# Retention heads: score products with the decay emitted ahead of the lo parts, and GpSimd's weight sums in halves

## The chip, the cores and the metric

The kernel runs on one core of one Trainium2 chip. The metric is the device time of one execution in microseconds (us). "Before" is the median of three runs. A profile is of one execution, with the name of each tile that an instruction reads and writes, and the line of the kernel that issued it. The engines are called PE (TensorE, matmuls; PEld its weight loads), DVE (VectorE), ACT (ScalarE), POOL (GpSimd) and SP (SyncE, which issues most DMAs).

## The reference, cut to what matters

One layer of a decoder: a normalised input of 512 tokens and 16 meta tokens goes through a combined projection `w_in`; four retention heads and sixteen stick-breaking heads run side by side; their gated outputs are merged and projected, and a SwiGLU FFN follows. All is float32. The change lies in the retention heads:

```python
scores = jnp.einsum('bhncd,bhnsd->bhncs', qc, kc) * decay[:, None]
inner = jnp.einsum('bhncs,bhnse->bhnce', scores, vc)
...
y_ret = head_groupnorm(retention_chunkwise(q_r, k_r, heads(rv, RET_HEADS)))
y_ret = (jax.nn.silu(rg.astype(jnp.float32)) * merge_heads(y_ret)).astype(dtype) @ w_ret_out
```

Each head has keys and queries of width 256 and values and a gate of width 512. The kernel computes a head's scores over the whole sequence at once, with one decay table for the causal triangle, in place of the reference's chunks with a carried state.

## The kernel before, in words

Matmuls of near-float32 accuracy are made of three products. Every operand is split into a hi part (`split`, L98: ACT copies it to the matmul format, L99) and a lo part (`lo_of`, L95: DVE subtracts the hi part from the source, L96); PE multiplies hi by hi, hi by lo and lo by hi. So for each weight or activation a DVE subtraction follows an ACT copy; all of them have the lines L99 and L96, and are told apart by their tiles: `wh`, `wl` are weights, `sh`, `sl` scores, `smt` the scores of the meta tokens.

The large projections of the retention heads use a scheme of seven products of half-size blocks in place of eight (`seven`, L260, numbered 0 to 6). It needs sums of the weights' quarters. `tok_quarters` (L230) loads a head's gate or value weights as two DMA tiles `raw` of 128x2048, splits the quarters, and has POOL form four sums of 128x1024 elements (L252 to L255): `y` and `x` go to tiles named `st`, the other two are made in place. They are split in turn (`wl<-st`, `wl<-raw`). It is called so for the gate of all four heads and for the values of heads 1 to 3; the values of head 0 are summed in place by other lines (L244 to L247). The results of the seven products are added into `ub` by DVE: L271, L274, L277 (which reads product 4, in a bank of the pool `b`) and L282.

A head's order in the program is: `ret_qk` (queries and keys, rotated), `tok_quarters` of the gate, `ret_scores`, `ret_gate`, `ret_pv` (scores times values, group norm, gating), `ret_T` (transposes), then `rv_proj` of the next head (its `tok_quarters` and seven products) and `ret_out`. In `ret_scores` each score block is a group of six matmuls into a PSUM bank `pb`; first the 16 meta rows (512 columns), then four blocks `j` of 128 rows with 512, 384, 256 and 128 columns. DVE multiplies the bank by the decay table into a tile `tm` (L941 for the meta rows, L953 for the blocks), and `tm` is split into hi and lo. In `ret_pv` the group of matmuls for token block `i` begins with the meta rows (`rvm`, `smt`) and then uses the blocks 0 to `i`.

Two rings set limits here. Score blocks, product 4 of the gate, and the groups of `ret_pv` share the two banks of the pool `b`. The tiles `tm` share a ring of three buffers, `rt`, with the temporaries of the rotation and of the group norm.

The order within each engine's queue is drawn up when the program is built: a planner goes through the instructions with its own estimate of their times and gives each engine, among those that are ready, the one emitted first. It fills a free engine with later work, so weights of the next head are split between the steps of this one. A few parts (the stick-breaking stage and the final product) are pinned to the order of the program; the retention heads are not. Once built, each engine runs its queue strictly in order.

Of the kernel before, what the change touches and what calls it, by code (L numbers as in the profile page):

```python
# [10 lines left out]
F32 = mybir.dt.float32  # L11
F32R = mybir.dt.float32r
AF = mybir.ActivationFunctionType
ALU = mybir.AluOpType
PSUM = bass.MemoryType.PSUM

P = 128
NM = 16
T = 512
L = NM + T  # L20
NT = T // P
# [13 lines left out]
def hybrid_block(  # L35
# [18 lines left out]
    nc = tc.nc  # L54
    x, out = x[0], out[0]
# [15 lines left out]
    def bank_b():  # L71
        return ps_b.tile([P, 512], F32, tag="b", name="pb")
# [16 lines left out]
    def mm(*args, **kw):  # L89
        return keep(nc.tensor.matmul(*args, **kw))  # L90
# [4 lines left out]
    def lo_of(lo, src, hi):  # L95
        nc.vector.tensor_tensor(lo, src, hi.bitcast(F32), op=ALU.subtract)  # L96

    def split(hi, lo, src):  # L98
        ins = nc.scalar.activation(hi, src, AF.Copy)  # L99
        if split_in_order[0]:  # L100
            tc.keep_in_program_order(ins)
        lo_of(lo, src, hi)
# [43 lines left out]
    H, KH = T // 2, KD // 2  # L146
# [43 lines left out]
    def wun_split(v):  # L190
        wh = wun.tile([P, v.shape[1], v.shape[2]], F32R, tag="wh", name="wh")
        wl = wun.tile([P, v.shape[1], v.shape[2]], F32R, tag="wl", name="wl")
        split(wh, wl, v)
        return wh, wl
# [35 lines left out]
    def tok_quarters(src, sums=None):  # L230

        raws = []
        for i in range(2):
            raw = wraw.tile([P, KH, 512], F32, tag="raw", name="raw")
            nc.sync.dma_start(raw, src[KH * P * i : KH * P * (i + 1), :].rearrange("(k p) c -> p k c", p=P))
            raws.append(raw)
        A11, A21 = raws[0][:, :, 0:256], raws[0][:, :, 256:]
        A12, A22 = raws[1][:, :, 0:256], raws[1][:, :, 256:]
        u = {}
        u["a11"] = wun_split(A11)  # L240
        u["a12"] = wun_split(A12)
        if sums is None:
            u["a22"] = wun_split(A22)
            nc.gpsimd.tensor_tensor(A22, A21, A22, op=ALU.add)  # L244
            nc.gpsimd.tensor_tensor(A21, A11, A21, op=ALU.subtract)
            nc.gpsimd.tensor_tensor(A11, A22, A11, op=ALU.subtract)
            nc.gpsimd.tensor_tensor(A12, A12, A11, op=ALU.subtract)  # L247
            u["s2"], u["s3"], u["s1"], u["s4"] = [wun_split(a) for a in (A11, A21, A22, A12)]
            return u
        x = sums.tile([P, KH, 256], F32, tag="st", name="st")  # L250
        y = sums.tile([P, KH, 256], F32, tag="st", name="st")
        nc.gpsimd.tensor_tensor(y, A11, A21, op=ALU.subtract)  # L252
        nc.gpsimd.tensor_tensor(A21, A21, A22, op=ALU.add)
        nc.gpsimd.tensor_tensor(x, A21, A11, op=ALU.subtract)  # L254
        nc.gpsimd.tensor_tensor(A12, A12, x, op=ALU.subtract)  # L255
        u["s2"], u["s3"], u["s1"] = wun_split(x), wun_split(y), wun_split(A21)
        u["s4"], u["a22"] = wun_split(A12), wun_split(A22)
        return u
# [563 lines left out]
    RT = 3  # L822
    s4 = s4c.enter_context(tc.tile_pool(name="s4", bufs=2, side=RS, reuse_waits="tile"))
# [11 lines left out]
    smt = s4.tile([80, T], F32R, name="smt", bufs=1)  # L835
# [26 lines left out]
    def rv_proj(h):  # L862
        u = tok_quarters(w_in[:, O_RV + DV * h : O_RV + DV * (h + 1)], s4 if h else None)
        ub = s4.tile([P, 4, 512], F32, tag="ub", name="ub", bufs=1)
        vs = s4.tile([P, L], F32, tag="rt", name="vs", bufs=RT)[:NM, :DV]

        def meta_part(n):

            c = 0 if n == 1 else 1
            ps, cs = bank_b()[:48, :256], slice(256 * c, 256 * (c + 1))  # L870
            ws = ((xm[:, 0:KH], u["a11"]), (xm[:, KH:KD], u["a12"])) if c == 0 else ((xm[:, 0:KH], u["s1"]), (xm2, u["a22"]))
            for i, (m, w) in enumerate(ws):
                for k in range(KH):
                    for j in range(2):
                        mm(ps, m[:, k, :], w[j][:, k, :], start=(i + j + k == 0), stop=(i == 1 and j == 1 and k == KH - 1))
            nc.scalar.activation(vs[:, cs], ps[32:48], AF.Copy)
            nc.vector.tensor_tensor(vs[:, cs], ps[0:16], vs[:, cs], op=ALU.add)

        tok_seven(u, tokens, ub, after=meta_part)
        vh = s4.tile([P, NT, DV], F32R, tag="vh", name="vh", bufs=1)  # L880
        vl = s4.tile([P, NT, DV], F32R, tag="vl", name="vl", bufs=1)
        for q in range(4):
            c, t = q // 2, q % 2
            dst = lambda v: v[:, 2 * t : 2 * t + 2, 256 * c : 256 * (c + 1)]
            split(dst(vh), dst(vl), ub[:, q, :].rearrange("p (a b) -> p a b", a=2))
        split(rvm[0:16, :], rvm[64:80, :], vs)
        nc.scalar.activation(rvm[32:48, :], rvm[0:16, :].bitcast(F32), AF.Copy)
        return [(vh[:, j, :], vl[:, j, :]) for j in range(NT)]
# [20 lines left out]
    def ret_qk(h):  # L909
        uq = feat_units(w_in[:, O_RQ + DK * h : O_RQ + DK * (h + 1)])  # L910
        pq = bank_a()
        for e in range(2):
            feat_mm(pq[:, e, :], uq[e], xtok, ltok)
        q = [(qk_tile(), qk_tile()) for _ in range(2)]
        idf = lambda t: t[:, :T]
        rotate(pq[:, 0, :], pq[:, 1, :], cosT[:, NM:], sinT[:, NM:], idf, [(a[:, :T], b[:, :T]) for a, b in q])
        uk = feat_units(w_in[:, O_RK + DK * h : O_RK + DK * (h + 1)])
        pks = []
        for e in range(2):
            pk = bank_a()  # L920
            for i in range(2):
                cs = slice(264 * i, 264 * (i + 1))
                feat_mm(pk[:, i, :264], uk[e], lambda k: hT[:, k, cs], lambda k: hL[:, k, cs])
            pks.append(pk[:, :, :264])
        k = [(qk_tile(), qk_tile()) for _ in range(2)]
        two = lambda t: t.rearrange("p (a b) -> p a b", a=2)
        rotate(pks[0], pks[1], two(cosT), two(sinT), two, [(two(a), two(b)) for a, b in k])
        return q, k

    def ret_scores(h, q, k):  # L930
        st = []
        dec = s4.tile([P, L], F32, tag="dec", name="dec", bufs=1)
        nc.sync.dma_start(dec, decay[h])
        pb = bank_b()
        n = 0
        for e in range(2):
            for a, b in ((0, 0), (0, 1), (1, 0)):
                mm(pb[:NM], k[e][a][:, 0:NM], q[e][b][:, :T], start=(n == 0), stop=(n == 5))
                n += 1
        tm = s4.tile([P, T], F32, tag="rt", name="tm", bufs=RT)  # L940
        nc.vector.tensor_tensor(tm[:NM], pb[:NM], dec[0:NM, NM:], op=ALU.mult)  # L941
        split(smt[0:16, :], smt[32:48, :], tm[:NM])
        nc.scalar.activation(smt[64:80, :], smt[0:16, :].bitcast(F32), AF.Copy)
        for j in range(NT):
            w = T - j * P
            pb = bank_b()
            n = 0
            for e in range(2):
                for a, b in ((0, 0), (0, 1), (1, 0)):
                    mm(pb[:, :w], k[e][a][:, NM + j * P : NM + (j + 1) * P], q[e][b][:, j * P : T], start=(n == 0), stop=(n == 5))  # L950
                    n += 1
            tm = s4.tile([P, T], F32, tag="rt", name="tm", bufs=RT)
            nc.vector.tensor_tensor(tm[:, :w], pb[:, :w], dec[:, :w], op=ALU.mult)  # L953
            sh = s4.tile([P, w], F32R, tag=f"sh{j}", name="sh", bufs=1)
            sl = s4.tile([P, w], F32R, tag=f"sl{j}", name="sl", bufs=1)
            split(sh, sl, tm[:, :w])
            st.append((sh, sl))
        return st

# [61 lines left out]
    for h in range(RH):  # L1021
        q, k = ret_qk(h)
        us = tok_quarters(w_in[:, O_RG + DV * h : O_RG + DV * (h + 1)], s4)
        st = ret_scores(h, q, k)
        gts = ret_gate(us)
        ret_pv(h, st, vts, us, gts)
# [46 lines left out]
    with tc.tile_pool(name="s6w", bufs=4, side=RS, reuse_waits="tile") as s6w, tc.tile_pool(  # L1073
        name="s6t", bufs=2, side=RS, reuse_waits="tile"
# [228 lines left out]
```

## Time and profile before

| what | value |
|---|---|
| time before, median of 3 runs (lowest, highest) | 1223.07 us (1222.41, 1224.04) |
| the profiled execution's own time | 1223.93 us |
| its span, first to last instruction | 1222.2 us |
| mean granted TensorE clock | 0.994 |
| busy: PE, DVE, ACT, POOL | 1173.2, 875.8, 534.0, 381.2 us |
| POOL's sums of L252 to L255 | 7 of each line, first start 379.7 us |
| decay products, L941 and L953 | 4 and 16 |

In the timeline, a row has the start in us, the duration in us (of all instructions that the row merges), the engine, the line, the operation, the tiles (out<-in), the shape and the count. A bracket at its end gives the idle time of the engine before it and what ended that. In the table of stretches, each engine's busy time is followed by its count of instructions; PEclk is the granted clock as a share of full speed. A busy PE is not a PE at its peak: at a lower granted clock the same matmuls take longer and count as busy.

### The profile page before, as it was taken

To read this page: it belongs to the slowest core of one execution; us is meant where nothing else is said; L and a number is where in the kernel's file an instruction comes from. 1 tells how busy PE (TensorE), PEld (TensorE's weight loads), DVE (VectorE), ACT (ScalarE), POOL (GpSimd) and SP (SyncE) were. 2 spreads that over 40 slices of the span, in tenths; PEclk is the share of its full clock that TensorE was granted. 3 is DMA by queue.
4 is the path that set the end of the run, shared out by engine and by line. 5 is a ranking of instruction groups with operands and counts; after the bars stand their busy time and mean duration, and the time that the engine had idled before them with its cause. 6 is when DMAs were issued, how large, how long until landed. Compare 5 with 4: busy or idle time off the path is not lost.

```text
span 1222.2 us, 18904 instructions
## 1 busy us (share of the span) xinstructions
PE 1173.2 (96%) x7629; PEld 1064.6 (87%) x7629; DVE 875.8 (72%) x1138; ACT 534.0 (44%) x873; POOL 381.2 (31%) x422
## 2 busy tenths in 40 slices
PE   7999998889999999989999999999999999999997
PEld 6888888788889988988898889778899999998886
DVE  6588888887537885586678747776889999984333
ACT  5476666655424434333332424334464444443221
POOL 2037767554033220230213030000256666630000
PEclk9999999999999999999999999999999999999999
DMA  6331111114643214122421424424223333343211
GB/s 192 87 95 44 53 52 56 49 44 144 222 139 110 70 45 137 35 80 71 134 70 45 138 69 121 143 107 155 70 70 105 104 104 104 105 163 130 85 53 69
DMA packets 94503, 118.25 MB, mean 97 GB/s; under 512 B 2488, under 2 KB 71104, under 8 KB 94416
## 3 DMA queue, kind: packets, MB, share of 16 engines
q1 hardware_dynamic: 93984, 115.98, 29.0%
q8 instruction: 60, 0.98, 0.3%
q10 hardware_dynamic: 432, 1.07, 0.3%
q14 instruction: 27, 0.22, 0.1%
HBM read 109.96 MB, written 7.08 MB: 96 GB/s over the span
## 4 chain that ended last, share of the span: by engine, by line
PE 74%; DVE 12%; ACT 3%; POOL 2%; DMA 2%; issue 2%; DVEq 0%; POOLq 0%; ACTq 0%; SPq 0%
PE pp L90 31%; PE pb L90 20%; PE pa L90 18%; PE pc L90 4%; DVE wl L96 2%; DVE sm L620 2%; PE pb L93 2%; DVE sp L621 2%; DVE sl L96 1%; ACT wh L99 1%; POOL mg L629 1%; DMA raw<-in_w_in_dram 1%; DVE kl L96 1%; DMA raw<-in_w_sb_out_dram 1%; POOL mg L630 1%
## 5 line engine op out<-in xcount | busy, mean ns | idle before, releaser
L96 DVE TENSOR_TENSOR wl<-raw,wh 128x1024 fp32r<-128x1024 f32 (+1 forms) x202 | 274.0, 1365 | 81.3 <-ACT wh L99 78.1
L99 ACT ACTIVATE wh<-raw 128x1024 fp32r<-128x1024 f32 (+1 forms) x202 | 201.4, 1007 | 261.3 <-PE pa L90 85.5
L90 PE MATMUL pp<-hT,wh 128*128 128x512 f32 (+2 forms) x308 | 108.7, 353 | 12.9 <-DVE qb L96 7.9
L90 PE MATMUL pp<-hL,wh 128*128 128x512 f32 (+2 forms) x308 | 103.5, 336 | 0.0
L90 PE MATMUL pp<-hT,wl 128*128 128x512 f32 (+2 forms) x308 | 103.4, 336 | 0.0
L96 DVE TENSOR_TENSOR wl<-st,wh 128x1024 fp32r<-128x1024 f32 x54 | 81.0, 1505 | 9.5 <-ACT wh L99 9.5
L90 PE MATMUL pp<-qk,wh 128*128 128x512 f32 x256 | 83.2, 399 | 2.0 <-ACT qk L99 1.7
L90 PE MATMUL pp<-wh,hT 128*128 128x256 f32 (+1 forms) x240 | 77.1, 322 | 2.5 <-DVE kl L96 1.8
L90 PE MATMUL pp<-wh,hL 128*128 128x256 f32 (+1 forms) x240 | 75.3, 314 | 0.8 <-DVE ss L142 0.8
L90 PEld LDWEIGHTS pp<-hT,wh 128*128 128x128 f32 x308 | 58.1, 189 | 20.2 <-issue 9.0
L90 PE MATMUL pp<-wl,hT 128*128 128x256 f32 (+1 forms) x240 | 75.1, 313 | 0.0
L99 ACT ACTIVATE wh<-st 128x1024 fp32r<-128x1024 f32 x54 | 56.0, 1055 | 35.5 <-POOL st L254 17.1
L252 POOL TENSOR_TENSOR st<-raw 128x1024 f32<-128x1024 f32 x7 | 17.2, 2461 | 166.8 <-DMA raw<-in_w_in_dram 166.8
L143 POOL TENSOR_TENSOR rs<-rs,nhalf 128x1 f32<-128x1 f32 x20 | 12.7, 634 | 181.2 <-DVE rs L142 181.2
L629 POOL CAST mg<-sp 128x16 fp32r<-128x16 f32 x64 | 31.1, 487 | 109.5 <-DVE sp L621 53.6
L90 PEld LDWEIGHTS pp<-hT,wl 128*128 128x128 f32 x308 | 58.0, 188 | 6.2
L90 PE MATMUL pa<-hL,wh 128*128 128x264 f32 (+1 forms) x192 | 61.6, 321 | 0.0
L620 DVE TENSOR_TENSOR_SCAN sm<-sm,mask 128x528 f32<-128x528 f32 (+1 forms) x64 | 59.7, 945 | 2.6 <-ACT sm L616 2.2
L90 PE MATMUL pa<-hT,wl 128*128 128x264 f32 (+1 forms) x192 | 61.6, 321 | 0.0
L90 PE MATMUL pa<-hT,wh 128*128 128x264 f32 (+1 forms) x192 | 61.6, 321 | 0.0
L90 PEld LDWEIGHTS pp<-hL,wh 128*128 128x128 f32 x308 | 58.2, 189 | 3.8
L90 PEld LDWEIGHTS pp<-qk,wh 128*128 128x128 f32 x256 | 47.6, 188 | 13.4 <-ACT qk L99 2.4
(334 smaller groups left out, 3847.7 us busy)
## 6 DMA issues: line engine op xcount, KB each, us to landing
raw<-in_w_in_dram SPq DMA_DIRECT2D x31, 1024.0 KB, 5.1
raw<-in_w_ffn_in_dram SPq DMA_DIRECT2D x22, 1024.0 KB, 5.1
raw<-in_w_in_dram SPq DMA_DIRECT2D x26, 512.0 KB, 4.1
raw<-in_w_ffn_out_dram SPq DMA_DIRECT2D x11, 1024.0 KB, 4.9
raw<-in_w_ret_out_dram SPq DMA_DIRECT2D x8, 1024.0 KB, 4.9
raw<-in_w_sb_out_dram SPq DMA_DIRECT2D x4, 1024.0 KB, 7.5
raw<-in_w_out_dram SPq DMA_DIRECT2D x4, 1024.0 KB, 5.1
ysb<-in_x_dram SPq DMA_DIRECT2D x4, 512.0 KB, 9.0
```

The lines of the kernel that those rows point to most:

```text
L90: return keep(nc.tensor.matmul(*args, **kw))
L93: return keep(nc.tensor.transpose(dst, src, idn))
L96: nc.vector.tensor_tensor(lo, src, hi.bitcast(F32), op=ALU.subtract)
L99: ins = nc.scalar.activation(hi, src, AF.Copy)
L143: nc.gpsimd.tensor_tensor(dst, dst, nhalf[:n], op=ALU.pow)
L252: nc.gpsimd.tensor_tensor(y, A11, A21, op=ALU.subtract)
L620: nc.vector.tensor_tensor_scan(rev, rev, mask[:, r0:][:, ::-1], 0.0, op0=ALU.mult, op1=ALU.max)
L621: nc.vector.tensor_tensor(sp, sp, sm[:, r0 + 1 : L + 1], op=ALU.mult)
L629: nc.gpsimd.tensor_copy(g[:, i, 0:NM], att[i][:, 0:NM])
L630: nc.gpsimd.tensor_tensor(g[:, i, NM:], att[i][:, 0:NM], g[:, i, 0:NM].bitcast(F32), op=ALU.subtract)
```

## The change

In `tok_quarters` each of POOL's four sums over 128x1024 elements becomes two over 128x512, one for each half of the four row blocks; the order of the four is kept. In `ret_scores` the five products with the decay are emitted in one loop, and the hi and lo parts of the four blocks in a second one after it. The split of the meta rows, which came straight after their product, is emitted ahead of block 2. Block 3 no longer takes a buffer of its own: its product is written to the columns of block 1's tile that the 384 columns leave free.

```diff
         x = sums.tile([P, KH, 256], F32, tag="st", name="st")
         y = sums.tile([P, KH, 256], F32, tag="st", name="st")
-        nc.gpsimd.tensor_tensor(y, A11, A21, op=ALU.subtract)
-        nc.gpsimd.tensor_tensor(A21, A21, A22, op=ALU.add)
-        nc.gpsimd.tensor_tensor(x, A21, A11, op=ALU.subtract)
-        nc.gpsimd.tensor_tensor(A12, A12, x, op=ALU.subtract)
+
+        for d, p, q, op in ((y, A11, A21, ALU.subtract), (A21, A21, A22, ALU.add), (x, A21, A11, ALU.subtract), (A12, A12, x, ALU.subtract)):
+            for k in range(0, KH, 2):
+                nc.gpsimd.tensor_tensor(d[:, k : k + 2], p[:, k : k + 2], q[:, k : k + 2], op=op)
...
-        tm = s4.tile([P, T], F32, tag="rt", name="tm", bufs=RT)
-        nc.vector.tensor_tensor(tm[:NM], pb[:NM], dec[0:NM, NM:], op=ALU.mult)
-        split(smt[0:16, :], smt[32:48, :], tm[:NM])
-        nc.scalar.activation(smt[64:80, :], smt[0:16, :].bitcast(F32), AF.Copy)
+        tmm = s4.tile([P, T], F32, tag="rt", name="tm", bufs=RT)
+        nc.vector.tensor_tensor(tmm[:NM], pb[:NM], dec[0:NM, NM:], op=ALU.mult)
+
+        tms = {}
         for j in range(NT):
+            if j == 2:
+                split(smt[0:16, :], smt[32:48, :], tmm[:NM])
+                nc.scalar.activation(smt[64:80, :], smt[0:16, :].bitcast(F32), AF.Copy)
             w = T - j * P
             pb = bank_b()
...
-            tm = s4.tile([P, T], F32, tag="rt", name="tm", bufs=RT)
-            nc.vector.tensor_tensor(tm[:, :w], pb[:, :w], dec[:, :w], op=ALU.mult)
+            if j < 3:
+                tm = s4.tile([P, T], F32, tag="rt", name="tm", bufs=RT)
+                tms[j] = tm[:, :w]
+            if j == 1:
+                tms[3] = tm[:, w : w + P]
+            nc.vector.tensor_tensor(tms[j], pb[:, :w], dec[:, :w], op=ALU.mult)
+        for j in range(NT):
+            w = T - j * P
             sh = s4.tile([P, w], F32R, tag=f"sh{j}", name="sh", bufs=1)
             sl = s4.tile([P, w], F32R, tag=f"sl{j}", name="sl", bufs=1)
-            split(sh, sl, tm[:, :w])
+            split(sh, sl, tms[j])
             st.append((sh, sl))
         return st
```

## The prediction

> **What bounds the kernel now.** I read the page's busy shares and chain first, then who makes TensorE (PE) wait in the retention part, then that place instruction by instruction.
>
> ```profile
> span 1222.2 us, 18904 instructions
> ...
> PE 1173.2 (96%) x7629; PEld 1064.6 (87%) x7629; DVE 875.8 (72%) x1138; ACT 534.0 (44%) x873; POOL 381.2 (31%) x422
> ...
> PE 74%; DVE 12%; ACT 3%; POOL 2%; DMA 2%; issue 2%; DVEq 0%; POOLq 0%; ACTq 0%; SPq 0%
> ```
>
> PE is the bound: a change in another engine's order pays only where PE stands still. In the retention part (376 to 742 us, three of the four heads) the list of waits has for PE just two entries (columns: total us, times, longest):
>
> ```profile
> PE pb L90 <- DVE tm L953: 8.0, 3, 3.4
> PE pp L90 <- ACT qk L99: 1.7, 3, 0.6
> ```
>
> The first is the line that the change moves: the product with the decay, `tm`, on VectorE (DVE). Once in each of heads 0, 1 and 2 PE waits for it at the first matmul of `ret_pv`, since that matmul writes the bank that the last `tm` still has to read. Timeline of PE (start us, duration us; in brackets the idle time and its releaser); the rows named `pb<-qk` are scores, those with `rvm,smt` begin the groups of `ret_pv`:
>
> ```profile
> 421.29 1.92 PE L90 MATMUL pb<-qk 128*128 128x384 f32 x12
> ...
> 426.89 0.78 PE L90 MATMUL pb<-qk 128*128 128x128 f32 x6
> ...
> 430.19 0.28 PE L90 MATMUL pb<-wl,th 128*128 128x256 f32 x1
> 430.31 0.28 PE L90 MATMUL pb<-wh,tl 128*128 128x256 f32 x1
> 432.88 0.47 PE L90 MATMUL pb<-rvm,smt 80*128 80x512 f32 x1 [2.29 <-DVE tm L953]
> ...
> 438.25 0.40 PE L90 MATMUL pb<-rvm,smt 80*128 80x512 f32 x1
> 438.48 0.39 PE L90 MATMUL pb<-vh,sh 128*128 128x512 f32 x1
> ...
> 442.71 0.28 PE L90 MATMUL pa<-wh,th 128*128 128x256 f32 x1
> ...
> 542.87 0.77 PE L90 MATMUL pb<-rvm,smt 80*128 80x512 f32 x1 [3.42 <-DVE tm L953]
> ...
> 651.42 0.47 PE L90 MATMUL pb<-rvm,smt 80*128 80x512 f32 x1 [2.25 <-DVE tm L953]
> ```
>
> Each wait has a second price. Busy time by stretch (columns: us; then busy us of PE, PEld, DVE, ACT, POOL with counts; granted clock; DMA share; GB/s): after each the clock is 0.69 to 0.71 for some 5.5 us, in this stage otherwise 1.00.
>
> ```profile
> 416.00:432.88 16.88, 14.59 (x116) 14.02 (x114) 16.74 (x15) 8.47 (x12) 9.66 (x4) 1.00 0.20 64
> 432.88:438.41 5.53, 5.53 (x29) 5.22 (x30) 5.53 (x7) 1.77 (x3) 0.00 (x0) 0.69 0.18 49
> 542.87:548.30 5.43, 5.43 (x29) 5.04 (x30) 5.43 (x7) 1.77 (x3) 0.00 (x0) 0.71 0.18 50
> 651.42:657.00 5.58, 5.58 (x29) 5.24 (x30) 5.58 (x7) 1.77 (x3) 0.00 (x0) 0.69 0.21 51
> 743.00:760.00 17.00, 17.00 (x124) 16.04 (x124) 12.41 (x17) 7.46 (x11) 0.00 (x0) 1.00 0.46 126
> 484.00:505.00 21.00, 21.00 (x102) 17.46 (x101) 6.10 (x7) 6.41 (x8) 10.66 (x4) 1.00 0.14 51
> ```
>
> Why is the last `tm` late? Its matmuls (128x128, x6) end at 427.67, but `tm` runs at 432.45. Timeline of DVE in head 0, then of GpSimd (POOL):
>
> ```profile
> 423.33 0.68 DVE L96 TENSOR_TENSOR sl<-tm,sh 128x512 fp32r<-128x512 f32 x1
> 423.93 0.88 DVE L953 TENSOR_TENSOR tm<-pb,dec 128x384 f32<-128x384 f32 x2
> 424.89 2.47 DVE L96 TENSOR_TENSOR wl<-raw,wh 128x1024 fp32r<-128x1024 f32 x1
> 427.28 5.25 DVE L96 TENSOR_TENSOR sl<-tm,sh 128x384 fp32r<-128x384 f32 x2
> 432.45 0.28 DVE L953 TENSOR_TENSOR tm<-pb,dec 128x128 f32<-128x128 f32 x1
> 432.65 2.34 DVE L96 TENSOR_TENSOR wl<-st,wh 128x1024 fp32r<-128x1024 f32 x2
> 434.92 0.28 DVE L96 TENSOR_TENSOR sl<-tm,sh 128x128 fp32r<-128x128 f32 x1
> 435.12 1.21 DVE L277 TENSOR_TENSOR ub<-pb,ub 128x1024 f32<-128x1024 f32 x1
> ```
>
> ```profile
> 423.87 2.41 POOL L253 TENSOR_TENSOR raw<-raw 128x1024 f32<-128x1024 f32 x1 [6.43 <-DMA raw<-in_w_in_dram]
> 426.35 3.25 POOL L254 TENSOR_TENSOR st<-raw 128x1024 f32<-128x1024 f32 x1
> 429.68 2.56 POOL L255 TENSOR_TENSOR raw<-raw,st 128x1024 f32<-128x1024 f32 x1
> ```
>
> Two lo parts (`sl`) stand ahead of it and take 5.25 us. In head 3, which has no such sums beside it, the same pair takes 0.89 and PE is busy 17.00 of 17.00 us:
>
> ```profile
> 752.33 0.88 DVE L953 TENSOR_TENSOR tm<-pb,dec 128x384 f32<-128x384 f32 x2
> ...
> 755.48 0.89 DVE L96 TENSOR_TENSOR sl<-tm,sh 128x384 fp32r<-128x384 f32 x2
> ```
>
> So DVE and POOL take turns, a whole instruction at a time: `wl` ends 427.36, 1.08 after L253's end at 426.28, and the `sl` pair ends 432.53, just after L255's end at 432.24. The two `tm` at 423.93 take 0.88 with L253 beside them as without it: an operation with one operand in PSUM isn't held up. The `wl` needs only about 1.17 itself (the pair at 432.65, when POOL is still, takes 2.34). Hence 5.25 - 0.89 = 4.36 us of the wait ahead of the last `tm` is POOL's.
>
> **The change part by part.**
>
> *Products ahead of the lo parts (4 heads).* No instruction more or less: 5 products, 5 hi and 5 lo parts as before, no DMA. The last `tm` lies in the free end of the second's tile. What moves is the order of emission, from which the planner draws up each queue; the trace of before can't show the new queues, so the cost is bounded. The five `tm` should come ahead of `sl` 0 to 3 on DVE, and the lo part of the meta rows, which sets a buffer free, stays ahead of the third. Head 0: the last score's matmuls end by 427.67 even if PE's order stays; `tm` then takes 0.28 and ends at 427.95. PE is free for `ret_pv` at 430.31 + 0.28 = 430.59, so the idle goes. If one held-up `sl` still stands ahead, it adds at most a half sum (1.29, below) and about 0.5: 429.8, still in time. Taken: 2.29 + 3.42 + 2.25 = 8.0 us of idle gone. Where nothing moves, it is 0.
>
> *The clock after it.* 5.53 x 0.31 + 5.43 x 0.29 + 5.58 x 0.31 = 5.0 us. An idle of 1.78 us elsewhere left the clock at 1.00, so what remains must be below something between 1.78 and 2.25:
>
> ```profile
> 184.72 0.36 PE L90 MATMUL pp<-hT,wh 128*128 128x264 f32 x1 [1.78 <-DVE qb L96]
> ```
>
> ```profile
> 184.70:186.70 2.00, 1.98 (x16) 2.00 (x17) 2.00 (x3) 1.65 (x3) 1.76 (x4) 1.00 0.79 232
> ```
>
> [...]
>
> *Sums in halves (7 groups: gate of 4 heads, value of heads 1 to 3).* 28 POOL instructions become 56. A half is as large as the sums of the FFN:
>
> ```profile
> 865.19 1.29 POOL L205 TENSOR_TENSOR st<-raw 128x512 f32<-128x512 f32 x1 [4.03 <-DMA raw<-in_w_ffn_in_dram]
> 866.45 2.28 POOL L207 TENSOR_TENSOR st<-raw 128x512 f32<-128x512 f32 x1
> ```
>
> 1.26 from start to start against 2.48 (423.87 to 426.35) for a whole: eight halves take 10.1 us, four wholes 9.9. The 0.2 per group is POOL's alone. A DVE operation now waits at most 1.29 for its turn instead of 2.4, but there are twice the turns, and a half that waits for DVE costs POOL about 1 (2.28 - 1.29). Up to three more such turns of 1.2 delay the later sums by 0 to 3.6 us. Behind them: ACT's hi part, DVE's `wl<-st` (done 434.99), PE's matmul with it at 442.71. The margin is 7.7, and 3.9 once PE comes about 3.9 earlier; I take nothing, the end being 0. The gate groups (as at 484 to 505) run while PE is busy 21.00 of 21.00 and DVE 6.10: nothing either.
>
> *What is late next.* After the first `ret_pv` group (4 matmuls at 0.23, 438.25 to 438.48) and 24 at 0.12 (430.19 to 430.31) PE reaches the second group at 430.59 + 0.92 + 2.88 = 434.39, before at 438.25. It needs the bank that L277 reads (435.12 to 436.33 before), and L277 stands behind two `wl<-st` and an `sl`. Best end: score banks freed early let the gate's product run ahead of other PE work, L277 ends by 434.4 and costs 0. Other end: from 427.95 DVE does all of `sl` 0 to 3 (0.68 + 0.89 + 0.28), both `wl<-st` (2.34) and L277 (1.21), 5.40 us, with the four halves of L254 and L255 in between (4 x 1.26): 438.4, idle 4.0. With the halves only and the queue as before, two halves ahead of the last `tm` (2.58 for 4.36) bring L277 to 434.5, or to 437.1 if the last two fall after it. I take 0.3 us a head, nearest to 434.5, since the banks' order lets L277 forward: 0.9.
>
> Head 3 has no sums; its lo parts come later, under a PE that is full and a DVE with 4.6 us free of 17: 0.
>
> Sum: 8.0 + 5.0 - 0.9 = 12.1 us. The profiled execution took 1223.93 (span 1222.2 and 1.7 around it), 0.86 above the median of 1223.07: 1211.8 against it, 1211.0 against the median.
>
> **The rivals.**
>
> *The wait moves to the second group, and L277 stays where it is.* It ends at 436.33, so PE gains 438.25 - 436.4 = 1.85 a head. The new idle of 2.0 lies between 1.78 (clock kept) and 2.25 (halved): 5.6 in all, 1217.5, or, with 1.7 of clock lost again, 0.15 a head, 1222.6. For it: DVE is busy 16.74 of 16.88 us, so its turns with POOL are shifted, not saved. Against it: L277 needs no turn. [...]
>
> *Slower: L277 falls behind all lo parts.* Its end of 438.4 above means 0.15 later than before at the second group and 1.7 us of slow clock after it, 1.85 a head: 1228.6. It decides from an end of 436.55 (438.25 less 1.7). For it: the lo parts are emitted ahead of the gate's products, so they have the prior claim. Against it: five `tm` leave the banks sooner, which calls L277's matmuls up too.
>
> *Nothing moves in effect:* the planner, which sets the queues from its own times, fills DVE with ready lo parts while the last score is still on PE, so `tm` stays behind them; the halves alone then leave an idle near 0.5 and move L277 by -1.8 to +0.8. That gives 1213 to 1223.
>
> **How the numbers follow.** Both waits gone (1209 to 1213): 0.50. Partly moved, clock kept (1213 to 1219): 0.27. L277 unmoved with the clock lost, or no effect (1213 to 1225, mostly above 1221): 0.12. Slower (1226 to 1229): 0.11. The first has the most because each part of the change by itself takes most of the first wait away, and the second wait needs L277 to stay behind work of lower claim. It gives 1211.0. The range of 1208.5 (all of 13.0 and 1.6 of the 1.7 us of waits on `qk`) to 1222 holds the first two, 0.77, and a part of the third. A measurement of this kernel tells about 0.2% (2.4 us) from no change: faster 0.79 (0.02 of it from the lower end of the no-effect case), same 0.10, slower 0.11.
>
> **What would show it.** Right: no PE wait on `tm` in heads 0 to 2, the granted clock at 1.00 between 430 and 440, the last `tm` in DVE's order ahead of `sl` of the wider scores, POOL's sums as 128x512 of 1.29 and up, DVE's `sl` no longer than about 2 us each. Wrong: a PE wait on L277 (`ub`) or `sl` at the second group with a clock near 0.7; PE waiting for `wl` of `st` at the product of 442.71; or the time from one head's first `ret_pv` group to the next (432.88, 542.87, 651.42: 109 us), not shorter by some 4 us.

## The result

The kernel after takes 1215.68 us (median of 6 runs, 1215.06 to 1216.34) and the kernel before, beside it on the same chip, 1223.51 (6 runs, 1222.41 to 1224.31). The ratio is 0.9933, with a 95% interval of 0.9922 to 0.9944: 7.8 us faster. The forecast was 1211.0, with a range of 1208.5 to 1222. The profiled execution of after took 1216.20, 7.7 less than that of before.

The page of after, its head, its busy times and the shares of the chain:

```profile
span 1214.1 us, 18932 instructions
...
PE 1169.6 (96%) x7629; PEld 1061.5 (87%) x7629; DVE 865.4 (71%) x1138; ACT 534.0 (44%) x873; POOL 396.4 (33%) x450
...
PE 75%; DVE 12%; POOL 4%; ACT 3%; DMA 3%; issue 2%; SPq 0%; DVEq 0%; POOLq 0%; ACTq 0%
```

PE is busy 3.6 us less with the same 7629 matmuls: that is clock, not work. Its mean granted clock rose from 0.994 to 0.997. POOL has 28 instructions more and 15.2 us more busy time (381.2 to 396.4), and PE waits nowhere for one of its sums. Next the list of waits of PE from 376 to 742 us, the view in which before had 8.0 us on `tm`:

```profile
PE pb L90 <- DVE ub L277: 3.3, 3, 1.1
PE pp L90 <- ACT qk L99: 1.7, 3, 0.6
```

The wait on `tm` is gone in all three heads. In its place stands a shorter one on L277, the gate's fourth product, at the second group of `ret_pv`. In head 0, by the timeline of PE, the first group starts with no bracket and the second waits 1.11 us:

```profile
431.46 0.40 PE L90 MATMUL pb<-rvm,smt 80*128 80x512 f32 x1
...
436.63 0.50 PE L90 MATMUL pb<-rvm,smt 80*128 80x512 f32 x1 [1.11 <-DVE ub L277]
```

The stretches that hold these groups, heads 0 to 2 (columns as before; the eighth number is the granted clock), show 1.00 where before had 0.69 to 0.71 for 5.5 us of each:

```profile
431.46:436.90 5.44, 4.33 (x32) 3.94 (x31) 5.29 (x5) 2.51 (x5) 2.69 (x2) 1.00 0.18 50
536.00:552.00 16.00, 14.86 (x106) 13.74 (x105) 13.96 (x21) 5.54 (x8) 5.47 (x5) 1.00 0.25 83
645.00:665.00 20.00, 18.91 (x131) 17.43 (x130) 17.00 (x28) 5.09 (x8) 3.60 (x5) 1.00 0.17 60
```

The surprise is in DVE's order. Timeline of DVE in head 0, then of POOL:

```profile
424.22 1.32 DVE L96 TENSOR_TENSOR sl<-tm,sh 128x512 fp32r<-128x512 f32 x1
425.46 0.88 DVE L960 TENSOR_TENSOR tm<-pb,dec 128x384 f32<-128x384 f32 x2
426.26 1.52 DVE L96 TENSOR_TENSOR wl<-raw,wh 128x1024 fp32r<-128x1024 f32 x1
427.70 3.06 DVE L96 TENSOR_TENSOR sl<-tm,sh 128x384 fp32r<-128x384 f32 x2
430.69 0.28 DVE L960 TENSOR_TENSOR tm<-pb,dec 128x128 f32<-128x128 f32 x1
431.61 3.63 DVE L96 TENSOR_TENSOR wl<-st,wh 128x1024 fp32r<-128x1024 f32 x2 [0.64 <-ACT wh L99]
435.16 0.28 DVE L96 TENSOR_TENSOR sl<-tm,sh 128x128 fp32r<-128x128 f32 x1
435.36 1.21 DVE L277 TENSOR_TENSOR ub<-pb,ub 128x1024 f32<-128x1024 f32 x1
```

```profile
423.69 3.00 POOL L255 TENSOR_TENSOR raw<-raw 128x512 f32<-128x512 f32 x2 [4.09 <-DVE smt L96]
426.65 3.83 POOL L255 TENSOR_TENSOR st<-raw 128x512 f32<-128x512 f32 x2
430.45 3.71 POOL L255 TENSOR_TENSOR raw<-raw,st 128x512 f32<-128x512 f32 x2
```

The order is that of before: over the whole kernel DVE, ACT and SP have the very same queues. On PE, in heads 0 to 2, a matmul of the projection beside it has moved ahead of each of the last three groups of `ret_pv`, and one among the transposes. Three `sl` and a `wl` still stand ahead of the last `tm`. What changed is durations. The pair of `sl` takes 3.06 instead of 5.25 and the `wl` 1.52 instead of 2.47, since each now waits for a half sum; the first `sl` (1.32 for 0.68) gives a little back. From the start of that `sl` to the last `tm` are 6.47 us instead of 9.12: 2.65 sooner, more than the wait of 2.29 (in heads 1 and 2 it is 3.74 and 2.71 sooner, against waits of 3.42 and 2.25). Behind it the turns come back: both `wl<-st` take 3.63 instead of 2.34, and 0.64 is idle ahead of them. L277 comes only 0.65 sooner on the same scale (11.14 for 11.79).

### The profile page after: what moved, and what is told of

It reads as the page before. It is cut to its first block, busy times and chain, and to the rows that moved or that the text cites. A ratio compares the mean times of both kernels' runs of the same rounds, so it can differ in the third digit from the quotient of the medians.

```text
span 1214.1 us, 18932 instructions
## 1 busy us (share of the span) xinstructions
PE 1169.6 (96%) x7629; PEld 1061.5 (87%) x7629; DVE 865.4 (71%) x1138; ACT 534.0 (44%) x873; POOL 396.4 (33%) x450
## 4 chain that ended last, share of the span: by engine, by line
PE 75%; DVE 12%; POOL 4%; ACT 3%; DMA 3%; issue 2%; SPq 0%; DVEq 0%; POOLq 0%; ACTq 0%
PE pp L90 31%; PE pb L90 20%; PE pa L90 18%; PE pc L90 4%; DVE wl L96 3%; DVE sm L620 3%; PE pb L93 2%; DVE sp L621 2%; ACT wh L99 1%; POOL mg L629 1%; DMA raw<-in_w_in_dram 1%; DMA ysb<-in_x_dram 1%; POOL raw L255 1%; DVE kl L96 1%; POOL st L255 1%
## 5 line engine op out<-in xcount | busy, mean ns | idle before, releaser
L96 DVE TENSOR_TENSOR wl<-raw,wh 128x1024 fp32r<-128x1024 f32 (+1 forms) x202 | 264.7, 1319 | 80.2 <-ACT wh L99 77.0
L255 POOL TENSOR_TENSOR st<-raw 128x512 f32<-128x512 f32 x28 | 44.8, 1620 | 164.8 <-DMA raw<-in_w_in_dram 164.8
L143 POOL TENSOR_TENSOR rs<-rs,nhalf 128x1 f32<-128x1 f32 x20 | 12.7, 634 | 170.7 <-DVE rs L142 170.7
```

What stands on the lines that cost most here:

```text
L143: nc.gpsimd.tensor_tensor(dst, dst, nhalf[:n], op=ALU.pow)
L255: nc.gpsimd.tensor_tensor(d[:, k : k + 2], p[:, k : k + 2], q[:, k : k + 2], op=op)
```

## The experiments

Theory A: the halves do it all, by shorter turns; the planner undoes the new order of emission; and what is left is L277's place in DVE's queue. Rivals were that the products' order helps, and that turns with POOL don't explain the long `sl`. Shown last: what an idle costs in clock.

**The halves alone.** The edit, on the kernel before:

```diff
-        nc.gpsimd.tensor_tensor(y, A11, A21, op=ALU.subtract)
...
+            for k in range(0, KH, 2):
+                nc.gpsimd.tensor_tensor(d[:, k : k + 2], p[:, k : k + 2], q[:, k : k + 2], op=op)
```

> Only GpSimd's sums are halved; the score products stay where they were. Theory A (the halves did all of it; the planner gives every engine the same queue with or without the products moved): 1215.7 us, within 1 us of the changed kernel; no PE wait on tm, a wait of about 1.1 us on L277 at the second ret_pv group in heads 0 to 2. Theory B (the products ahead of the lo parts carry a part, as the prediction had it): 1218 to 1221 us, with PE still waiting for tm.

Measured: 1215.22 us (1214.75 to 1216.42), ratio 0.9930 (0.9917 to 0.9942), the gain of the whole change. Its queues are those of after on every engine. The waits of PE in the same window (L276 is L277 here):

```profile
PE pb L90 <- DVE ub L276: 3.6, 3, 1.3
PE pp L90 <- ACT qk L99: 1.7, 3, 0.6
```

**The products alone.** The edit, on the kernel after, is the inverse of the one above: whole sums again.

> Only the score products are emitted ahead of the lo parts; the sums stay whole. Theory A: 1223.5 us, same as before, with PE's three waits on tm of 2.3 to 3.4 us and a clock near 0.7 after each. Theory B: 1215 to 1220 us, waits on tm gone or well under 2 us.

Measured: 1224.97 (1221.28 to 1226.08), ratio 1.0001 (0.9991 to 1.0010). Its queues are those of before, and its list of waits is nearly the same:

```profile
PE pb L90 <- DVE tm L960: 7.8, 3, 3.1
PE pp L90 <- ACT qk L99: 1.7, 3, 0.6
```

So the halves are the change, and the products' part of it does nothing.

**Which halves.** The gate's sums whole again, on the kernel of the halves alone (`step` is 2 for the values):

```diff
-        us = tok_quarters(w_in[:, O_RG + DV * h : O_RG + DV * (h + 1)], s4)
+        us = tok_quarters(w_in[:, O_RG + DV * h : O_RG + DV * (h + 1)], s4, KH)
```

> The kernel before with the sums in halves for the value weights only (heads 1 to 3); the gate's sums (four heads) stay whole. All queues but GpSimd's are the same as in e1_halves_only. Theory A (only the sums that run beside the scores matter; the gate's run while PE is busy throughout, 21.00 of 21.00 us): as e1, 1214.5 to 1216.5, with the wait on L277 of 1.0 to 1.3 us a head and none on tm. Rival (halving the gate's sums helps too, by shorter turns that bring DVE's other work forward): 0.5 to 3 us slower than e1's 1215.2.

Measured: 1216.57 (1214.18 to 1216.90), ratio 0.9930 (0.9915 to 0.9946), with 3.4 us of waits on L277 in three heads and none on `tm`. The ratio is that of the halves alone; the median lies 1.35 us above theirs, but the median of before beside it is 0.8 higher too. So the sums of heads 1 to 3's values, which run beside the scores of the head before, are the ones that matter.

**Is it turns?** On the kernel before, the four sums of each group are left out, and fills of the same tiles stand in their place:

```diff
-        nc.gpsimd.tensor_tensor(y, A11, A21, op=ALU.subtract)
...
+        nc.gpsimd.memset(y, 0.0)
...
```

> The kernel before, with the four sums of each group on GpSimd replaced by four fills with zero of the same 128x1024 tiles: GpSimd writes as much as before but reads nothing (the sums of the weights are left out; everything else is done). Theory A (DVE's lo part waits because GpSimd's two-operand sum and its own two-operand subtraction take turns): no turn to take, so the pair of sl that took 5.25 us takes 0.89 in all heads, no DVE lo part of 1024 columns is over 1.3, PE waits for tm nowhere in 376 to 742, and the second group's wait on L277 is at most 0.3; 1208 to 1212. Rival (any use of memory by GpSimd blocks DVE, writes too, or the lo parts are long for a reason of their own such as the store of their result): the pair stays at 2 to 5 us where a fill lies beside it, the tm wait stays at 1 to 3 us a head, and the time at 1217 to 1224.

Measured in one run: 1212.01 us. DVE, then POOL, head 0:

```profile
427.18 1.22 DVE L96 TENSOR_TENSOR wl<-st,wh 128x1024 fp32r<-128x1024 f32 x1
428.31 0.89 DVE L96 TENSOR_TENSOR sl<-tm,sh 128x384 fp32r<-128x384 f32 x2
429.12 0.29 DVE L953 TENSOR_TENSOR tm<-pb,dec 128x128 f32<-128x128 f32 x1
```

```profile
427.37 0.95 POOL L255 MEMSET raw<- 128x1024 f32 x1 [10.34 <-DVE wl L96]
428.46 0.95 POOL L252 MEMSET st<- 128x1024 f32 x1
```

A fill runs beside each of the first two DVE rows, and both take what they take alone (1.22, and 0.89 as in head 3 of before). Over 376 to 742 us none of DVE's lo parts takes more than 1.23. So it is neither the `sl` itself nor POOL's writing that holds DVE up, but something that the sums have and the fills lack; they read two operands, the fills none. PE waits for neither `tm` nor L277, and 12.7 us are gone from the 1224.66 of before beside it (1221.86 to 1227.10), near the forecast's 13.0 for idle and clock together. DVE's queue is not quite that of before: the `wl<-st` shown has moved ahead of the pair, so the time is not a measure of the turns alone.

**The products truly ahead.** In the kernel with the products alone, the lo parts of the scores are made to queue behind the last product:

```diff
-            nc.vector.tensor_tensor(tms[j], ...)
+            last = nc.vector.tensor_tensor(tms[j], ...)
...
-            split(sh, sl, tms[j])
+            nc.scalar.activation(sh, tms[j], AF.Copy)
+            with tc.issue_after(last.ins):
+                lo_of(sl, tms[j], sh)
```

> Whole sums, but the lo parts of the scores really queued behind the last score product on VectorE. Theory A (VectorE's turns with GpSimd are only moved by this, since the sums take as long): no PE wait on tm, but L277 ends near 436.2 in head 0 and PE waits about 1.8 us at the second ret_pv group: 1217.5 us if the clock stays, 1222.5 if it halves after that wait. Theory B (the prediction's first step: products ahead end the stall by themselves): 1211 to 1213 us, no wait over 0.5 us.

Measured: 1224.02 (1218.55 to 1225.01), ratio 0.9992 (0.9981 to 1.0003). `tm` comes at 425.82 and is never waited for, but the three `sl` behind it take 5.63 us and L277 falls late:

```profile
425.82 0.29 DVE L960 TENSOR_TENSOR tm<-pb,dec 128x128 f32<-128x128 f32 x1
426.03 5.63 DVE L96 TENSOR_TENSOR sl<-tm,sh 128x512 fp32r<-128x512 f32 x3
...
432.92 1.21 DVE L277 TENSOR_TENSOR ub<-pb,ub 128x1024 f32<-128x1024 f32 x1
```

The waits on L277 are 1.47, 2.53 and 1.47. With whole sums the turns are moved from one side of `tm` to the other, and PE meets them one group later.

**The same with the halves,** both parts of the change as it is worded:

> Both parts of the change as they are worded: the sums in halves, and the lo parts of the scores queued behind the last product with the decay on DVE (as in e5_forced_whole, whose other queues it shares). The forecast's own step: no wait on tm, and at the second group's wait on L277 between 0 and 4.0 us a head, 0.3 taken: 1211 or a little under. Theory A (turns are moved, not saved: all lo parts of scores and of the sums run between the last tm and L277, as in e5, but in half turns): tm never waited for, L277 waited for 0.5 to 1.5 us a head, clock at 1.00 or lost after one or two; 1212 to 1217, no better than the halves alone (1215.2). Rival (the wait on L277 is as long as with whole sums, 1.5 to 2.5, since the sum of the turns is the same): 1218 to 1224.

Measured: 1216.49 (1215.83 to 1217.88), ratio 0.9934 (0.9921 to 0.9948), as the halves alone. In the retention part it is better: L277 is waited for 0.79, 0.62 and 0.62 instead of 1.1 each. It is given back near 860 us, where the planner, starting from this new order, has drawn up DVE's queue otherwise around the tile `mix` (a `wl` that is idle 4.02 us for its hi part on ACT now stands ahead of the product of L1128, which is L1126 in after and ran ahead of it). Waits of PE from 764 us to the end, first after, then this kernel:

```profile
PE pb L93 <- DVE mix L1141: 1.1, 1, 1.1
```

```profile
PE pb L93 <- DVE mix L1128: 1.6, 1, 1.6
PE pb L93 <- DVE tl L96: 0.9, 1, 0.9
PE pb L93 <- DVE rs L142: 0.8, 1, 0.8
```

3.3 us for 1.1. The whole-sum kernel above has the same three (1.4, 0.9, 0.8), so some 2 us of its time are lost there and not in the heads.

**L277 first.** In the kernel after, the lo parts of the next head's `st` tiles queue behind L277:

```diff
+            with tc.issue_after(behind.ins) if behind is not None else ExitStack():
+                lo_of(wl, v, wh)
...
+        fourth[0] = nc.vector.tensor_tensor(ub[:, 1:4:2, :], ...)
...
-        u = tok_quarters(w_in[:, O_RV + ...], s4 if h else None)
+        u = tok_quarters(w_in[:, O_RV + ...], s4 if h else None, fourth[0])
```

> The changed kernel, with VectorE's lo parts of the two st tiles of the next head's values queued behind L277. Theory A (what is left is the wait of 1.1 us a head on L277, which stands behind those two lo parts): the waits at the second ret_pv group go, 3 x 1.1 us less than the changed kernel, about 1212.4 us. Rival C (VectorE and GpSimd together are the bound there, so the wait passes to the next thing that VectorE owes PE): 1215 to 1216.5 us, with a new PE wait on wl of st or on a lo part of the scores.

Measured: 1208.92 (1208.50 to 1210.88), ratio 0.9879 (0.9866 to 0.9892). PE waits for nothing at all from 376 to 742 us. DVE in head 0: L277 (here L286) follows the last `sl`, and both `wl<-st` behind it meet no sum:

```profile
429.05 0.28 DVE L969 TENSOR_TENSOR tm<-pb,dec 128x128 f32<-128x128 f32 x1
431.12 0.57 DVE L97 TENSOR_TENSOR sl<-tm,sh 128x128 fp32r<-128x128 f32 x1 [1.79 <-ACT sh L100]
431.61 1.21 DVE L286 TENSOR_TENSOR ub<-pb,ub 128x1024 f32<-128x1024 f32 x1
432.75 2.34 DVE L97 TENSOR_TENSOR wl<-st,wh 128x1024 fp32r<-128x1024 f32 x2
```

It gained more than expected: besides 3.3 us on L277 the three waits on `qk` (1.7) went, which I had not foreseen. That is most of the 6.8 us between the medians (6.6 by the ratios). Of the 7.8 us between the spans of the two profiled executions, 5.9 arise from the start of head 0's scores to head 3's first group (333.2 us against 339.1), and 1.65 ahead of that, mostly where after lost clock (below). This is the best version.

**Are the halves then still needed?** The same kernel with whole sums; every queue but POOL's is the same:

> The changed kernel with L277 queued ahead of the lo parts of the sums (as in e4_fourth_first), but with the sums on GpSimd whole again. Every other queue is the same as in e4, so it tells whether the halves are still needed when L277 stands first. Theory A (the halves are what shortens the wait ahead of the last tm, L277's place only removes the second wait): tm waits as before, 2.3 to 3.4 us a head at the first group, the clock falls after most of them, no wait at the second group; 1221 to 1224, as the kernel before. Rival (putting L277 first sorts the turns so that one big sum does no harm): the tm wait is below 1 us, and the time is within 3 us of e4's 1208.9.

Measured: 1222.12 (1220.61 to 1223.27), ratio 0.9978 (0.9970 to 0.9987), with

```profile
PE pb L91 <- DVE tm L970: 7.6, 3, 3.0
```

They are. The wait on `tm` is back whole. Of the 2.5 us between the medians 1.7 are the waits on `qk`, which stay away.

**Both orders forced, with the halves:**

> e4_fourth_first (sums in halves, L277 ahead of the lo parts of the sums) with the lo parts of the scores also queued behind the last product. Theory A (e4 has no PE wait left in the retention part to take away, so an earlier tm gains nothing): within 2 us of e4's 1208.9, no wait on tm or L277 over 0.5. Rival (the lo parts of the scores, now later, are waited for by the first groups, which use them, or hold L277 up): a wait on sl or ub of 0.5 to 1.5 us a head; 1211 to 1216.

Measured: 1213.67 (1211.88 to 1215.47), ratio 0.9910 (0.9896 to 0.9924), 4.8 behind the best by the medians, 3.8 by the ratios. Both forms of what was expected fell short: no wait on `tm`, `sl` or L277 is left and 0.7 on `qk`, yet it isn't within 2 us. From 764 us on it waits 1.0, 0.9 and 0.8 on the same three tiles as above, and behind the last of them (0.97 us) the clock fell:

```profile
869.77:875.27 5.50, 5.19 (x26) 4.56 (x27) 3.66 (x6) 1.19 (x2) 0.00 (x0) 0.70 0.00 0
```

The spans of this profiled execution and of the best version's differ by 7.0 us, and by the start times of PE's matmuls 4.6 of these arise between 840 and 870 us: the price of the forced order is paid far behind the heads, in idle and in clock. The clock also fell at 183 to 190 us (0.76), but by 200 us that is made up. Another 1.5 us arise before 60 us, and their cause is open.

**What an idle costs in clock.** The kernel with the products truly ahead and whole sums, once more:

> The same kernel as e5_forced_whole once more, for a second trace of the same waits on L277 (1.47, 2.53, 1.47 us). [...] Rival (the length of the idle alone decides): the clock stays at 1.00 behind all three whatever the time, and the 6 us between the executions of this kernel are lost elsewhere.

Measured: 1225.32, waits on L277 of 1.75, 2.52 and 1.59. The stretches behind the three waits, first of the earlier execution (1218.55, waits 1.47, 2.53, 1.47), then of this one:

```profile
434.19:439.70 5.51, 5.51 (x39) 5.21 (x40) 5.16 (x10) 2.36 (x4) 0.77 (x2) 1.00 0.04 3
542.20:547.70 5.50, 5.50 (x39) 5.19 (x40) 5.15 (x10) 2.37 (x4) 0.75 (x2) 1.00 0.08 9
648.60:654.10 5.50, 5.50 (x39) 5.20 (x40) 5.15 (x10) 2.36 (x4) 0.76 (x2) 1.00 0.03 2
```

```profile
437.48:443.00 5.52, 5.52 (x27) 5.05 (x28) 5.17 (x10) 2.35 (x4) 0.77 (x2) 0.69 0.06 4
547.02:552.50 5.48, 5.48 (x26) 4.96 (x27) 5.13 (x10) 2.36 (x4) 0.73 (x2) 0.69 0.08 8
655.07:660.60 5.53, 5.53 (x40) 5.23 (x41) 5.18 (x10) 2.37 (x4) 0.78 (x2) 1.00 0.03 2
```

A wait of 2.53 kept the clock at 1.00 in one execution; one of 2.52 at the same instruction let it fall in the other, and so did one of 1.75. By the start times of its matmuls PE falls 1.8 and 1.6 us further behind at these two places (0.3 of it is the longer first wait), and 1.5 near 71 us, where idles of 1.71 and 0.92 us stand and the clock fell as well (0.76 from 73 to 80 us). So the clock has most of the 6.8 us between the two executions, not all.

## Why the prediction came out as it did

**Idle and clock of the first wait (8.0 and 5.0): right in size.** Both are gone, by the waits and the stretches shown.

**"The five `tm` should come ahead of `sl` 0 to 3 on DVE": wrong.** The planner kept the old order, as the rival "Nothing moves in effect" said: it fills DVE with ready lo parts while the last score is on PE. The products alone measured 1.0001. What removed the wait is the step that I had set down as costing nothing, and as one that would leave an idle near 0.5 if it stood alone: it left none, since the last `tm` came 2.65 sooner against a wait of 2.29. So the time fell inside that rival's 1213 to 1223, by its mechanism, and the forecast's likeliest case had the sign right and its first step wrong.

**"What is late next": the right wait, the wrong size.** L277 at the second group was taken at 0.3 us a head and measured 1.1, 3.3 in all against 0.9. PE's arrival was right: forecast 434.39; measured 435.52, less 0.89 by which that place runs late in this execution (the first `sl` starts at 424.22, before at 423.33), is 434.63. L277's end was not: forecast 434.5 (437.1 at the other end), measured 436.57 - 0.89 = 435.7. The working let the sums' last turns fall ahead of the last `tm`; one of them fell on the `wl<-st` pair behind it (3.63 - 2.34 = 1.29). That is the rival's "shifted, not saved" in part. Ahead of `tm` 2.65 us were saved, and 2.0 came back before L277. The time from one head's first group to the next is 106.18 and 106.07 us, 3.8 and 2.5 shorter, where the forecast looked for some 4. No run shows what sets the turns: the whole sums, which read two operands, held the pair of `sl` at 5.25 us, the halves at 3.06, and the fills, which read none, left it at 0.89.

**Its clock: right, but not for its reason.** A wait of 1.1 cost no clock in the three heads, and neither did the six waits of 1.05 to 1.30 with the halves alone and with the value halves. But "something between 1.78 and 2.25" as the threshold fell. Behind waits of 0.97 (both orders forced), 1.75 and 2.52 the clock fell, and behind 2.53 and 2.27 it did not. That the waits of 1.1 cost nothing was therefore in part luck. The stretch behind the 2.27:

```profile
651.14:656.60 5.46, 5.46 (x35) 5.00 (x36) 5.23 (x6) 1.78 (x3) 0.00 (x0) 1.00 0.20 53
```

It is the third wait on `tm` of the kernel with L277 first and whole sums; the stretches behind the other two, 2.37 and 2.95, have 0.69. What decides it no run shows. The length alone does not: at one instruction an idle of 2.53 left the clock at 1.00 in one execution and one of 2.52 was followed by 0.69 in the other, and 0.97 was followed by 0.70 where 2.27 left 1.00.

**The rest of the miss.** The sum was 12.1 against the profile of before; 7.7 came. L277 is 2.4 of the 4.4 missing. Another 1.0 was lost far ahead of the change: behind idles of 1.71 and 0.92 us in the stick-breaking stage (before: 1.42 and 0.92) the clock fell, and this stretch, which ran at 1.00 before, shows

```profile
72.00:80.00 8.00, 7.08 (x41) 6.63 (x40) 6.86 (x13) 3.35 (x7) 1.72 (x6) 0.79 0.07 20
```

PE is 1.5 us later than before at the end of this stretch, and 1.03 at the start of head 0's scores. The first group of head 3 starts at 752.87 against 760.84: 7.97 sooner. So the heads gave 9.0 of the 9.7 that waits and clock account for (8.0 + 5.0 - 3.3). Of the last 1.0, 0.4 lies outside the span of the instructions (the time is 2.1 us longer than the span in after, 1.7 in before), and for the 0.7 in the heads no row stands out.

**Gate groups, POOL's extra turns, head 3: right.** The gate's halves made no measurable difference (ratio 0.9930 with and without them), and PE waits nowhere for `wl` of `st`.

## What to carry to other kernels

Where two engines take turns on large operations, cut the one that is off the critical path: here the pair of `sl` took 3.06 us in place of 5.25 when the sums went from 128x1024 to 128x512, though 2.0 of the 2.65 us saved came back at the next consumer. Emitting something earlier is no reordering where a planner draws up the queues; compare the built queues first, then force the one consumer that PE waits for, and look at the far end of the kernel for what the planner moved in return. A short idle of PE had a price in clock that came out differently in two executions of one kernel (1.00 behind 2.53 us, 0.69 behind 2.52), so aim to take the idle away, not to bring its length under some threshold.

## What the runs showed of the hardware

A GpSimd fill of 128x1024 (0.95 us) ran inside DVE's subtraction at no cost, where GpSimd sums of that size held each of two smaller ones up by 2.2 (the pair of `sl` before: 5.25 us beside them, 0.89 without). TensorE's granted clock fell (0.69 over the next 5.5 us) behind an idle of 1.75 us and stayed at 1.00 behind one of 2.53, in two executions of one kernel; in another kernel it fell (0.70) behind one of 0.97.
